# Low weight halves added from HBM one unit earlier, and input stacks moved from GpSimd's queue to SyncE's

## The chip, the cores and the metric

One core of a Trainium2 chip runs the whole kernel. The metric is device time in microseconds (us), the median of three runs. A profiled execution, taken beside them, gives the trace.

## The reference, cut to what matters

A trunk of two layers works on 272 tokens (16 learned meta tokens and 256 of the input) of width 1024, in float32:

```
for l in range(2):
    h = h + 0.5 * swiglu(rmsnorm(h, g_ffn1[l]), w1_gate[l], w1_up[l], w1_down[l])   # width 2816
    z = rmsnorm(h, g_mix[l]) @ w_in[l]            # u, q, k, v, forget logits, gates
    y_a = s5_mixer(u, ...)                        # 32 groups of 16 channels, 64 complex states each
    y_b = forgetting_attention(q, k, v, f_logit)  # 8 heads of 64
    merged = gates_a * (y_a @ w_br_a[l]) + gates_b * (y_b @ w_br_b[l])
    h = h + merged @ w_o[l]
    h = h + 0.5 * swiglu(rmsnorm(h, g_ffn2[l]), w2_gate[l], w2_up[l], w2_down[l])
return rmsnorm(h[:, 16:], g_final)
```

In s5_mixer each group of 16 channels of u is multiplied by the complex matrices B, runs through a diagonal recurrence over the 272 tokens, and is multiplied by C; then come a gelu and a gated projection.

## The kernel before

Tokens lie along the free dimension, 272 columns; the width lies in blocks of 128 partitions. Every product with a weight is made of three passes of float32r matmuls: a weight tile w is split into hi = round(w) and lo = w - hi, activations likewise, and `unit` issues hi\*hi (L309), hi\*lo (L310) and lo\*hi (L311) for each of 8 blocks of the contraction. Weights are read once, as a stream of 378 units, 189 a layer, most of 128 x 1024 numbers. A unit is thus 24 matmuls.

The class `Weights` feeds the stream. `load` issues a transfer of one unit into a `raw` tile (four of them) from SyncE's queue (SP). `high` has ScalarE copy raw into a rounded `wh` tile (five). `low` makes the `wl` tile (four): VectorE subtracts (L182), or, for every second unit from 70 to 110 of a layer save the small unit 72, 20 a layer (`by_dma`), ScalarE writes -hi (L177) and GpSimd's queue (POOL) issues a transfer that adds raw to it from SBUF (L178).

The order of the work is written out: every engine and queue takes its instructions in the order of the program. After each unit `tick` runs: `W.high()` for the unit four ahead, then whatever was put off to this tick with `later`, then `W.low()` for the unit three ahead, then a piece of a background generator, measured out by a credit per tick (`budget`). Closures in `mids` are run inside the next unit, before its seventh block.

A layer is FFN, mixer, FFN. In the mixer, units 68 to 71 make u, 72 the forget logits, 73 to 76 v, 77 to 84 k and q, 85 to 100 the gates (with the attention between them), 101 and 102 two of branch b, 103 to 106 the gated projection, 107 to 112 the rest of both branches, 113 to 120 the output projection.

`have_u` scales a block m of u (four of them), splits it into uh and ul, and `done` builds an input stack x: for each quarter q (32 rows) three transfers of 32 x 272 numbers from SBUF to SBUF, uh, ul and uh below each other (L776), twelve a block and 48 a layer, all on POOL. Stack m is ready for use (`us[m]`) two ticks later for m = 0. The background generator `ssm_branch` asks for the product of step j (16 of them; j = 4m + q) with the state weights: `bu(j)`, two matmuls (L656) with 96 rows. Bs holds B rounded in its first 64 rows and B - round(B) in its last 32. VectorE then turns, scans and turns back (L678, L731, L733, L743), and `out_m` (L668) multiplies four steps with C.

`ssm_tables`, the background work of the FFN before, fills Bs in four parts of 1024 columns: a load of B from SP, copies of the first 64 rows and the rounded last 32 on ScalarE, and a subtraction on VectorE (L563), which takes 1200 of the credit. `halves` is a pool of 19 SBUF slots of 128 x 4 x 272 numbers, which activations, stacks and intermediate results take and give back in the order of the program.

Of the kernel before, what the change touches and what calls it, by code (L numbers as in the profile page):

```python
# [15 lines left out]
P = 128  # L16
# [23 lines left out]
WARM = 10  # L40
START = 8
BLOCK = 1024
DMA_LOW = (2 * NF + 3 * KD + 1, 2 * NF + 3 * KD + 43)
BROWS = 96
DELAY = 2
MASKED = -float(2.0 ** 100)
O_U, O_Q, O_K, O_V, O_F, O_G = 0, 512, 1024, 1536, 2048, 2056
MAGIC = 12582912.0
# [82 lines left out]
class Weights:  # L131
# [17 lines left out]
    def high(self, parts=1):  # L149
        i, nc = self.nh, self.nc  # L150
        if i >= len(WHERE):
            return
        b, c, w = WHERE[i]
        while self.nb <= min(b + RAW - 1, len(BLOCKS) - 1):
            self.load()
        r = self.raw[b][:, c : c + w]
        hi = self.pool.tile([P, D], F32R, tag="wh", name=f"wh{i}", bufs=LEAD + 1)
        for c in range(0, w, w // parts):
            nc.scalar.copy(hi[:, c : c + w // parts], r[:, c : c + w // parts])  # L159
        self.part[i] = (hi, r)  # L160
        self.nh += 1

    @staticmethod
    def by_dma(i):
# [4 lines left out]
    def low(self, parts=1):  # L169
        i, nc = self.nl, self.nc  # L170
        if i >= len(WHERE):
            return
        w = WHERE[i][2]
        hi, r = self.part[i]
        lo = self.pool.tile([P, D], F32R, tag="wl", name=f"wl{i}", bufs=LEAD)
        if self.by_dma(i):
            nc.scalar.activation(lo[:, :w], hi[:, :w].bitcast(F32), AF.Copy, scale=-1.0)  # L177
            nc.gpsimd.dma_start(lo[:, :w], r, accum_op=ALU.add)  # L178
            parts = 0
        for c in range(0, w, w // parts) if parts else ():  # L180
            k = slice(c, c + w // parts)
            nc.vector.tensor_sub(lo[:, k], r[:, k], hi[:, k].bitcast(F32))  # L182
        self.part[i] = (hi, lo)
        self.nl += 1
# [7 lines left out]
def body(tc, nc, ins, out):  # L192
    v, s, pe = nc.vector, nc.scalar, nc.tensor

    with (
# [7 lines left out]
    ):  # L203
        names = iter(range(10**6))

        halves = Slots(mp, "m", 19, [P, 4, T])
        banks = Slots(pp, "ps", 6, [P, 512])
        temps = Slots(tp, "t", 6, [P, T])
        bank, tmp = banks.take, temps.take
# [1 line left out]
        def big(n, dt=F32):  # L211
            return Tiles(halves, n, dt)
# [30 lines left out]
            return par[:, c : c + n]  # L243


        state = {"tick": 0, "bg": None, "credit": 0.0, "budget": FFN_BUDGET}
        queue, tails, mids = [], [], []
        tail = tails.append

# [299 lines left out]
        def ssm_tables(l):  # L549
# [2 lines left out]
            top = BROWS - 32  # L552
            for j in range(0, NJ, 4):
                x = Bs[:, j : j + 4].rearrange("p j c -> p (j c)")
                slots = halves.take(), halves.take(F32R)
                raw, hi = (y.rearrange("p a t -> p (a t)")[:BROWS, : 8 * P] for y in slots)
                nc.sync.dma_start(raw, ins["B"][l][:, j * 2 * P : (j + 4) * 2 * P])
                yield -1
                yield -1
                s.copy(x[:top], raw[:top])  # L560
                s.copy(hi[top:], raw[top:])
                yield -1
                v.tensor_sub(x[top:], raw[top:], hi[top:].bitcast(F32))  # L563
                yield 1200
                halves.give(*slots)
            cslot = halves.take()
            Cm = cslot.rearrange("p a t -> p (a t)")[:, : 2 * NJ * 32].rearrange("p (r j c) -> p r j c", r=2, j=NJ)
            nc.sync.dma_start(Cm, ins["C"][l])
# [80 lines left out]
        def ssm_branch(l, us, yr, t0):  # L649
            n = T - t0  # L650

            def bu(j):
                pb = bp.tile([P, 2, 512], F32, tag="b2", name=f"bu{next(names)}")
                m, q = divmod(j, 4)
                for r in range(2):
                    pe.matmul(pb[:, r, :T], lhsT=Bs[:, j, r * P : r * P + P], rhs=us[m](q)[:BROWS], start=True, stop=True)  # L656
                if q == 3:
                    us[m].give()
                return pb

            def out_m(m, qt):
                ps = bank()
                for x, row, a, b, start, stop in (
                    (0, 0, t0, T, True, False), (0, 3, t0, TS, False, False), (3, 2, t0, TS, False, False),
                    (1, 3, TS, T, False, False), (2, 2, TS, T, False, False), (2, 1, t0, T, False, True),
                ):
                    for q in range(4):
                        pe.matmul(  # L668
                            ps[32 * q : 32 * q + 32, a - t0 : b - t0], lhsT=Cx[:, x, 4 * m + q, :],
                            rhs=qt[q][:, row, a:b], start=start, stop=stop,  # L670
                        )
                return ps

            def turn(dst, x, j):

                d = dst.rearrange("p (k r) t -> p k r t", k=2)
                for a, tab in ((0, E[:, :, j, 1:][:, :, ::-1]), (TS, E[:, :, j, :TS])):
                    v.tensor_tensor(  # L678
                        d[:, :, :, a : a + TS], x[:, :, a : a + TS].unsqueeze(1).to_broadcast([P, 2, 2, TS]),
                        tab.unsqueeze(2).to_broadcast([P, 2, 2, TS]), ALU.mult,  # L680
                    )
                    yield 635

            pbs = {}

            def ask(j):
                mids.append(lambda: pbs.__setitem__(j, bu(j)))

            def shut(m, qt):


                def finish():
                    if not banks.free:
                        mids.append(finish)
                        return
                    ps = out_m(m, qt)
                    halves.give(*qt)

                    def store():
                        y = yr(m)[:, t0:]  # L700
                        v.scalar_tensor_tensor(y, y, pc("d", l, m), ps[:, :n], ALU.mult, ALU.add)
                        stored.append(m)
                        banks.give(ps)

                    later(1, store)

                mids.append(finish)

            while 0 not in us:
                yield -1  # L710
            ask(0)
            g, qt = None, []
            for j in range(NJ + 1):
                back = iter(())
                if j < NJ:
                    p = buf("p", 1, [P, 4, T])
                    while j not in pbs:
                        yield -1
                    yield from turn(p, pbs.pop(j)[:, :, :T], j)
                    if j + 1 < NJ:  # L720
                        assert (j + 1) // 4 in us
                        ask(j + 1)
                if j:
                    while not halves.free:
                        yield -1
                    qt.append(halves.take())
                    back = turn(qt[-1], g, j - 1)
                    yield next(back)
                if j < NJ:
                    c, d = (x.rearrange("p r (s t) -> p (r s) t", s=2) for x in (p[:, :2], p[:, 2:]))  # L730
                    v.tensor_add(c[:, 1:3], c[:, 1:3], d[:, 3::-3])  # L731
                    yield 352
                    v.tensor_sub(c[:, 0::3], c[:, 0::3], d[:, 2:0:-1])  # L733
                    yield 352
                yield from back
                if j and j % 4 == 0:
                    shut(j // 4 - 1, qt)
                    qt = []
                if j < NJ:
                    g = buf("g", 1, [P, 2, T])  # L740
                    mg = ssm["mag"][:, l * NJ + j : l * NJ + j + 1].to_broadcast([P, T])
                    for r in range(2):
                        v.tensor_tensor_scan(g[:, r], mg, p[:, r], 0.0, ALU.mult, ALU.add)  # L743
                        yield 352
# [7 lines left out]
        def mixer(l, hh, hl, t0, finish):  # L752
# [15 lines left out]
            def have_u(ps, m):  # L768

                scaled(ps, yr(m), 0)  # L770

                def done():
                    x = big(4, F32R)
                    for q in range(4):
                        for i, part in enumerate((uh, ul, uh)):
                            nc.gpsimd.dma_start(  # L776
                                x(q)[32 * i : 32 * i + 32].bitcast(F32), part(m)[32 * q : 32 * q + 32].bitcast(F32)
                            )
                    later(DELAY if m == 0 else 0, lambda: us.__setitem__(m, x))
                    if m == 3:  # L780
                        uh.give()
                        ul.give()

                split(uh(m), ul(m), yr(m), done)

# [272 lines left out]

            bias(0)
            yb = None  # L1060
            gB, gA = big(8), None
            for i in range(16):
                state["budget"] = GATE_BUDGET if i < 11 else LATE_BUDGET
# [16 lines left out]
                later(1, e)  # L1080
                if 5 <= i < 12 and i % 2 == 1:
                    yb = yb or big(8, F32R)
                    values((i - 5) // 2)
                if 3 <= i < 11:
                    flip(i - 3)
# [372 lines left out]
```

## Time and profile before

| | |
|---|---|
| median of three runs | 1267.73 us (1265.53 to 1271.29) |
| profiled execution | 1266.69 us, of which the span is 1264.9 |
| granted clock of TensorE, mean | 0.975 |
| TensorE, busy | 1202.2 us, 95% |
| VectorE, busy | 894.1 us, 71% |
| ScalarE, busy | 682.9 us, 54% |
| GpSimd, busy | 88.0 us, 7% |
| read from HBM | 198.75 MB, 158 GB/s over the span |

Shares are means over stages that differ: the three FFN stretches keep TensorE at 100%, the mixers don't. A mixer lies at about 208 to 451 us, and again at 848 to 1072.

### The profile page before, as it was taken

The page shows a single profiled execution, that of the slowest core. Times are in us where ns is not written, and L with a number is a line of the kernel's source. Part 1 is how long each engine was busy: PE and PEld are TensorE (multiplying, and loading weights), DVE is VectorE, ACT ScalarE, POOL GpSimd, SP SyncE. Part 2 cuts the span into 40 slices and gives each one's busy share as a digit, 9 for nine tenths or more (in the row PEclk, how much of TensorE's full clock was granted, in tenths as well). Part 3 has the DMA queues.
Part 4 walks back from the last instruction along what each step waited for, and adds up shares of the span by engine and source line. Part 5 has one row for each costly group of instructions (what it writes and reads, how often), then busy time and mean ns, then how long its engine had stood idle before and what let it go on. Part 6 is the DMA issues. An engine that isn't in the chain of part 4 may idle for free.

```text
span 1264.9 us, 24220 instructions
## 1 busy us (share of the span) xinstructions
PE 1202.2 (95%) x9753; PEld 1178.7 (93%) x9753; DVE 894.1 (71%) x1682; ACT 682.9 (54%) x1092; POOL 88.0 (7%) x148
## 2 busy tenths in 40 slices
PE   9999999589997999999999999996899889999997
PEld 8999999588887999999999999996888789999997
DVE  6967899379885867989665555554797867766553
ACT  7555444446766556544454444445467665544542
POOL 0000000710010000000000000008000000000000
PEclk9999999789998999999999999997899999999999
DMA  6766555677567656655556565555766675655561
GB/s 235 210 204 207 172 171 139 163 195 185 140 166 183 189 186 208 196 168 170 172 174 187 169 179 161 182 164 160 196 184 166 168 201 183 202 185 191 176 185 63
DMA packets 65921, 225.70 MB, mean 178 GB/s; under 512 B 8560, under 2 KB 8944, under 8 KB 65808
## 3 DMA queue, kind: packets, MB, share of 16 engines
q1 hardware_dynamic: 56480, 199.06, 49.9%
q0 software_dynamic: 8912, 24.47, 10.1%
q8 instruction: 76, 1.25, 0.4%
q10 hardware_dynamic: 416, 0.62, 0.1%
q14 instruction: 37, 0.30, 0.1%
HBM read 198.75 MB, written 1.05 MB: 158 GB/s over the span
## 4 chain that ended last, share of the span: by engine, by line
PE 81%; DVE 7%; DMA 5%; issue 3%; POOL 2%; ACT 1%; SPq 0%; DVEq 0%; POOLq 0%; ACTq 0%
PE ps L311 26%; PE ps L309 26%; PE ps L310 25%; DMA wl<-raw 3%; POOL m L776 2%; DMA raw<-wts 1%; DVE wl L182 1%; DVE g L743 1%; DMA m<-m 1%; DVE m L678 1%; DVE p L678 1%; PE ps L668 1%; PE ps L976 1%; PE bu L656 0%; DVE p L731 0%
## 5 line engine op out<-in xcount | busy, mean ns | idle before, releaser
L311 PE MATMUL ps<-m,wl 128*128 128x272 f32 (+2 forms) x2960 | 858.0, 290 | 47.2 <-DMA wl<-raw 45.8
L309 PE MATMUL ps<-m,wh 128*128 128x272 f32 (+2 forms) x2960 | 860.0, 291 | 0.4 <-ACT wh L159 0.4
L310 PE MATMUL ps<-m,wh 128*128 128x272 f32 (+2 forms) x2960 | 853.3, 288 | 0.3
L159 ACT CAST wh<-raw 128x1024 fp32r<-128x1024 f32 (+2 forms) x380 | 388.9, 1024 | 446.7 <-issue 211.5
L311 PEld LDWEIGHTS ps<-m,wl 128*128 128x128 f32 (+1 forms) x2960 | 563.4, 190 | 50.8 <-DMA wl<-raw 48.3
L309 PEld LDWEIGHTS ps<-m,wh 128*128 128x128 f32 (+1 forms) x2960 | 563.5, 190 | 5.4 <-issue 3.3
L310 PEld LDWEIGHTS ps<-m,wh 128*128 128x128 f32 (+1 forms) x2960 | 563.2, 190 | 1.2 <-DVE m L345 0.7
L182 DVE TENSOR_TENSOR wl<-raw,wh 128x1024 fp32r<-128x1024 f32 (+2 forms) x340 | 401.8, 1182 | 60.0 <-PE ps L311 41.3
L178 POOL DMA_DIRECT2D wl<-raw x40 | 34.9, 882 | 912.5 <-ACT wl L177 781.5
L402 DVE TENSOR_TENSOR t<-t,ps 128x272 f32<-128x272 f32 (+1 forms) x88 | 38.1, 433 | 76.3 <-PE ps L311 73.6
L678 DVE TENSOR_TENSOR p<-bu,E 128x544 f32<-128x544 f32 x64 | 44.3, 721 | 46.1 <-PE bu L656 43.6
L396 DVE TENSOR_TENSOR t<-ps,rstd 128x272 f32<-128x272 f32 (+1 forms) x88 | 38.3, 435 | 41.3 <-PE ps L311 40.7
L776 POOL DMA_DIRECT2D m<-m x96 | 47.8, 548 | 26.5 <-ACT m L325 18.5
L678 DVE TENSOR_TENSOR m<-g,E 128x544 f32<-128x544 f32 x64 | 45.9, 718 | 0.1
L743 DVE TENSOR_TENSOR_SCAN g<-ssm_mag,p 128x272 f32<-128x272 f32 x64 | 43.3, 712 | 0.9
L404 ACT CAST m<-t 128x272 fp32r<-128x272 f32 (+1 forms) x88 | 36.2, 411 | 13.6 <-DVE t L402 13.4
L397 ACT ACTIVATE t<-t 128x272 f32<-128x272 f32 (+1 forms) x88 | 37.2, 423 | 9.2 <-DVE t L396 8.7
L177 ACT ACTIVATE wl<-wh 128x1024 fp32r<-128x1024 f32 x40 | 42.1, 1052 | 0.0
L407 DVE TENSOR_TENSOR m<-t,m 128x272 fp32r<-128x272 f32 (+1 forms) x88 | 38.0, 432 | 3.8 <-ACT m L404 3.7
L430 DVE TENSOR_TENSOR t<-ps,rstd 128x272 f32<-128x272 f32 (+1 forms) x32 | 14.0, 437 | 37.7 <-PE ps L311 37.7
L342 ACT ACTIVATE m<-h,par 128x272 fp32r<-128x272 f32 (+1 forms) x48 | 24.5, 518 | 10.8 <-DVE h L432 5.3
L345 DVE SCALAR_TENSOR_TENSOR m<-h,par,m 128x272 fp32r<-128x272 f32 (+1 forms) x48 | 23.4, 494 | 8.3 <-ACT m L342 8.2
(220 smaller groups left out, 695.2 us busy)
## 6 DMA issues: line engine op xcount, KB each, us to landing
raw<-wts SPq DMA_DIRECT2D x344, 512.0 KB, 3.9
wl<-raw POOLq DMA_DIRECT2D x40, 512.0 KB, 5.3
raw<-wts SPq DMA_DIRECT2D x32, 384.0 KB, 3.1
m<-m POOLq DMA_DIRECT2D x96, 34.0 KB, 2.8
m<-B SPq DMA_DIRECT2D x8, 384.0 KB, 5.2
h<-hT SPq DMA_DIRECT2D x4, 272.0 KB, 5.4
m<-C SPq DMA_DIRECT2D x2, 512.0 KB, 4.5
out<-m SPq DMA_DIRECT2D x2, 256.0 KB, 2.1
```

The lines of the kernel that those rows point to most:

```text
L159: nc.scalar.copy(hi[:, c : c + w // parts], r[:, c : c + w // parts])
L177: nc.scalar.activation(lo[:, :w], hi[:, :w].bitcast(F32), AF.Copy, scale=-1.0)
L182: nc.vector.tensor_sub(lo[:, k], r[:, k], hi[:, k].bitcast(F32))
L309: pe.matmul(ps[:width, :n], lhsT=a, rhs=mh, start=first and i == ks[0], stop=False)
L310: pe.matmul(ps[:width, :n], lhsT=a, rhs=ml, start=False, stop=False)
L311: pe.matmul(ps[:width, :n], lhsT=b, rhs=mh, start=False, stop=last and i == ks[-1])
L396: v.tensor_mul(x[:, :n], pg[:, :n], rstd[:, t0:])
L402: v.tensor_mul(y[:, :n], y[:, :n], pu[:, :n])
L407: v.tensor_sub(al(f)[:, t0:], y[:, :n], ah(f)[:, t0:].bitcast(F32))
L678: v.tensor_tensor(d[:, :, :, a : a + TS], x[:, :, a : a + TS].unsqueeze(1).to_broadcast([P, 2, 2, TS]), tab.unsqueeze(2).to_broadcast([P, ...
L743: v.tensor_tensor_scan(g[:, r], mg, p[:, r], 0.0, ALU.mult, ALU.add)
L776: nc.gpsimd.dma_start(x(q)[32 * i : 32 * i + 32].bitcast(F32), part(m)[32 * q : 32 * q + 32].bitcast(F32))
```

## The change

- `high` makes the low half of the 40 units of `by_dma` at once, one tick earlier than `low` did; the added operand comes from the weights in HBM and no longer from raw. `low` passes over such a unit. There are five wl tiles in place of four.
- The stack transfers go out on SP. `put` issues three for one quarter, and the quarters of a block are spread over ticks by `STACKS`; uh and ul are given back with the last quarter. A quarter is ready for use one tick after its issue, and `us` goes by step j.
- The last 32 rows of Bs are -round(B), written by ScalarE, with B added from HBM by a transfer on POOL; the subtraction, its credit and one slot go.
- `halves` has 18 slots; from the gates' start until yb is taken, the generator leaves two free.

```diff
+LOWS = LEAD + 1
-DELAY = 2
+DELAY = 1
+STACKS = (0, 1, 4, 7)
@@ Weights.high
         self.nh += 1
+        if self.by_dma(i):
+            lo = self.pool.tile([P, D], F32R, tag="wl", name=f"wl{i}", bufs=LOWS)
+            nc.scalar.activation(lo[:, :w], hi[:, :w].bitcast(F32), AF.Copy, scale=-1.0)
+            off, n = BLOCKS[b]
+            src = self.dram[off * P : (off + n) * P].rearrange("(p n) -> p n", p=P)
+            c = WHERE[i][1]
+            nc.gpsimd.dma_start(lo[:, :w], src[:, c : c + w], accum_op=ALU.add)
+            self.part[i] = (hi, lo)
@@ Weights.low
+        if self.by_dma(i):
+            self.nl += 1
+            return
-        lo = self.pool.tile([P, D], F32R, tag="wl", name=f"wl{i}", bufs=LEAD)
-        if self.by_dma(i):
-            nc.scalar.activation(lo[:, :w], hi[:, :w].bitcast(F32), AF.Copy, scale=-1.0)
-            nc.gpsimd.dma_start(lo[:, :w], r, accum_op=ALU.add)
-            parts = 0
+        lo = self.pool.tile([P, D], F32R, tag="wl", name=f"wl{i}", bufs=LOWS)
@@ body
-        halves = Slots(mp, "m", 19, [P, 4, T])
+        halves = Slots(mp, "m", 18, [P, 4, T])
@@ ssm_tables
-                slots = halves.take(), halves.take(F32R)
+                slot = halves.take()
                 s.copy(x[:top], raw[:top])
-                s.copy(hi[top:], raw[top:])
+                s.activation(x[top:], raw[top:], AF.Copy, scale=-1.0)
+                nc.gpsimd.dma_start(x[top:], src[top:], accum_op=ALU.add)
+                halves.give(slot)
                 yield -1
-                v.tensor_sub(x[top:], raw[top:], hi[top:].bitcast(F32))
-                yield 1200
-                halves.give(*slots)
@@ ssm_branch
-                        assert (j + 1) // 4 in us
+                        while j + 1 not in us:
+                            yield -1
-                    while not halves.free:
+                    while len(halves.free) <= state["keep"]:
@@ mixer
+                def put(q, x):
+                    for i, part in enumerate((uh, ul, uh)):
+                        nc.sync.dma_start(
+                            x(q)[32 * i : 32 * i + 32].bitcast(F32), part(m)[32 * q : 32 * q + 32].bitcast(F32)
+                        )
+                    later(DELAY, lambda: us.__setitem__(4 * m + q, x))
+                    if q == 3 and m == 3:
+                        uh.give()
+                        ul.give()
                 def done():
                     x = big(4, F32R)
+                    first = state["tick"]
                     for q in range(4):
-                        for i, part in enumerate((uh, ul, uh)):
-                            nc.gpsimd.dma_start(
-                                x(q)[32 * i : 32 * i + 32].bitcast(F32), part(m)[32 * q : 32 * q + 32].bitcast(F32)
-                            )
-                    later(DELAY if m == 0 else 0, lambda: us.__setitem__(m, x))
-                    if m == 3:
-                        uh.give()
-                        ul.give()
+                        at = first + (q // 2 if m == 0 else q) + STACKS[m]
+                        queue.append((at, lambda q=q: put(q, x)))
             bias(0)
+            state["keep"] = 2
                     yb = yb or big(8, F32R)
+                    state["keep"] = 0
```

## Rows read from the trace of the kernel before

**Rows 1.** The page: busy time of each engine, share, instructions.

```profile
PE 1202.2 (95%) x9753; PEld 1178.7 (93%) x9753; DVE 894.1 (71%) x1682; ACT 682.9 (54%) x1092; POOL 88.0 (7%) x148
```

**Rows 2.** Waits of TensorE, whole span: waiter <- releaser, us in total, times, longest.

```profile
PE ps L311 <- DMA wl<-raw: 45.8, 11, 14.0
...
PE bu L656 <- DVE p L678: 1.5, 2, 0.8
```

**Rows 3.** The first of these waits at 200:300, 300:420, 840:900 and 900:1050 us.

```profile
PE ps L311 <- DMA wl<-raw: 18.6, 2, 14.0
...
PE ps L311 <- DMA wl<-raw: 6.8, 2, 3.4
...
PE ps L311 <- DMA wl<-raw: 13.6, 2, 9.8
...
PE ps L311 <- DMA wl<-raw: 6.7, 5, 2.1
```

**Rows 4.** Windows of 8 us after a stall, first and last of seven (PEclk before DMA share).

```profile
243.20:251.20 8.00, 7.98 (x44) 7.98 (x45) 3.43 (x6) 2.29 (x3) 7.03 (x15) 0.65 0.48 130
...
1026.70:1034.70 8.00, 7.44 (x48) 7.24 (x48) 4.82 (x11) 3.69 (x6) 0.86 (x1) 0.79 0.78 199
```

**Rows 5.** Timeline of POOL, 200 to 256 us: adding transfers of units 74 and 76.

```profile
238.04 0.91 POOL L178 DMA_DIRECT2D wl<-raw  x1 [0.25 <-issue]
...
252.75 1.83 POOL L178 DMA_DIRECT2D wl<-raw  x2 [0.21 <-issue]
```

**Rows 6.** Timeline of ScalarE: copy and negation of units 74 and 108; three sigmoids.

```profile
217.62 1.05 ACT L159 CAST wh<-raw 128x1024 fp32r<-128x1024 f32 x1 [1.02 <-DMA raw<-wts]
...
224.75 1.05 ACT L177 ACTIVATE wl<-wh 128x1024 fp32r<-128x1024 f32 x1
...
389.46 1.05 ACT L159 CAST wh<-raw 128x1024 fp32r<-128x1024 f32 x1 [3.04 <-PE ps L310]
...
391.25 1.35 ACT L1101 ACTIVATE m<-m,par 128x272 f32<-128x272 f32 x3 [0.45 <-DVE m L1100]
...
394.06 1.04 ACT L177 ACTIVATE wl<-wh 128x1024 fp32r<-128x1024 f32 x1
```

**Rows 7.** Timeline of POOL: the adding transfer of unit 108.

```profile
395.50 0.86 POOL L178 DMA_DIRECT2D wl<-raw  x1 [10.47 <-ACT m L1101]
```

**Rows 8.** Transfers: count, KB, median us to landing; below, the range for wl.

```profile
raw<-wts SPq DMA_DIRECT2D x344, 512.0 KB, 3.9
wl<-raw POOLq DMA_DIRECT2D x40, 512.0 KB, 5.3
...
m<-m POOLq DMA_DIRECT2D x96, 34.0 KB, 2.8
...
DMA to landing us min/median/max: 4.5/5.3/8.8
```

**Rows 9.** Timeline of SP at the start: two issues back to back.

```profile
1.65 0.90 SPq L224 DMA_DIRECT2D h<-hT  x2
```

**Rows 10.** Windows: length, busy us of PE, PEld, DVE, ACT, POOL, then PEclk.

```profile
210.90:218.30 7.40, 7.40 (x58) 7.21 (x57) 7.06 (x21) 3.27 (x4) 0.60 (x1) 1.00 0.48 116
262.65:283.00 20.35, 20.35 (x165) 20.29 (x164) 16.97 (x30) 12.77 (x22) 2.58 (x3) 1.00 0.70 183
229.00:378.80 149.80, 128.84 (x1119) 119.50 (x1117) 111.30 (x207) 89.88 (x183) 32.77 (x55) 0.92 0.65 167
660.00:680.00 20.00, 20.00 (x160) 20.00 (x160) 12.47 (x19) 10.28 (x16) 0.00 (x0) 1.00 0.69 215
```

**Rows 11.** VectorE: its wait for the stack products; the state weights' subtraction (xcount | busy, mean).

```profile
DVE p L678 <- PE bu L656: 43.6, 8, 16.5
...
L563 DVE TENSOR_TENSOR Bs<-m,m 32x1024 fp32r<-32x1024 f32 x8 | 9.7, 1218 | 11.1 <-ACT m L561 11.0
```

**Rows 12.** Timeline: VectorE makes ul of blocks 0 and 1; TensorE starts unit 73.

```profile
223.26 0.79 DVE L328 TENSOR_TENSOR m<-m,m 128x272 fp32r<-128x272 f32 x2
...
225.65 0.37 PE L309 MATMUL ps<-m,wh 128*128 128x272 f32 x1
```

More of the change, by code (lines that the diff above doesn't have):

```diff
@@ L172, in low @@
             return
+        if self.by_dma(i):
+            self.nl += 1
+            return
         w = WHERE[i][2]
         hi, r = self.part[i]
-        lo = self.pool.tile([P, D], F32R, tag="wl", name=f"wl{i}", bufs=LEAD)
-        if self.by_dma(i):
-            nc.scalar.activation(lo[:, :w], hi[:, :w].bitcast(F32), AF.Copy, scale=-1.0)
-            nc.gpsimd.dma_start(lo[:, :w], r, accum_op=ALU.add)
-            parts = 0
-        for c in range(0, w, w // parts) if parts else ():
+        lo = self.pool.tile([P, D], F32R, tag="wl", name=f"wl{i}", bufs=LOWS)
+        for c in range(0, w, w // parts):
             k = slice(c, c + w // parts)
@@ L243, in pc @@
             return par[:, c : c + n]
-        state = {"tick": 0, "bg": None, "credit": 0.0, "budget": FFN_BUDGET}
+        state = {"tick": 0, "bg": None, "credit": 0.0, "budget": FFN_BUDGET, "keep": 0}
         queue, tails, mids = [], [], []
@@ L554, in ssm_tables @@
                 x = Bs[:, j : j + 4].rearrange("p j c -> p (j c)")
-                slots = halves.take(), halves.take(F32R)
-                raw, hi = (y.rearrange("p a t -> p (a t)")[:BROWS, : 8 * P] for y in slots)
-                nc.sync.dma_start(raw, ins["B"][l][:, j * 2 * P : (j + 4) * 2 * P])
+                slot = halves.take()
+                raw = slot.rearrange("p a t -> p (a t)")[:BROWS, : 8 * P]
+                src = ins["B"][l][:, j * 2 * P : (j + 4) * 2 * P]
+                nc.sync.dma_start(raw, src)
                 yield -1
@@ L655, in bu @@
                 for r in range(2):
-                    pe.matmul(pb[:, r, :T], lhsT=Bs[:, j, r * P : r * P + P], rhs=us[m](q)[:BROWS], start=True, stop=True)
+                    pe.matmul(pb[:, r, :T], lhsT=Bs[:, j, r * P : r * P + P], rhs=us[j](q)[:BROWS], start=True, stop=True)
                 if q == 3:
-                    us[m].give()
+                    us[j].give()
                 return pb
```

## The prediction

> **What bounds the kernel now.** I read the page first: TensorE is busy 95% of the span [rows 1], so what can be won lies in the 5% and in the clock. Next came what TensorE waits for. Nearly all of it is one thing, the low half of a weight that an adding transfer makes: 45.8 us in 11 waits; the next in question, the state product waiting for VectorE, has 1.5 [rows 2]. Split by stretch, the waits lie in the mixers only: 18.6 us where the first begins, 6.8 where it ends, 13.6 and 6.7 in the second [rows 3]. Then the clock behind these waits. Behind seven of the eleven waits TensorE resumes at a granted clock of 0.50, its 1.2 GHz level, and is back at 2.4 GHz some us later: over the 8 us behind each the mean is 0.61 to 0.79 [rows 4]. One minus it, summed over the seven, is 2.20, so work at half speed cost 2.20 x 8 = 17.6 us. Elsewhere it is 1.00 [rows 10]. Waits and clock together are 63.4 us, the most that this cause can give back.
>
> Why is the transfer late? At the start, unit 74's ScalarE part ends at 225.8 (224.75 + 1.05) [rows 6], but POOL issues the addition at 238.04, and unit 76's at 252.75 [rows 5]: between stand stack transfers in the order of the program, 24 of them in these 14.7 us, 0.6 us each. POOL is busy 7% over the span, and yet its order is the bound there. At the mixer's end POOL is free. Unit 108's copy ends at 390.5, its negation waits in ScalarE's order until 394.06 [rows 6], POOL issues at 395.50 [rows 7], and a landing takes 4.5 to 8.8 us [rows 8]; TensorE got there 3.4 us too early.
>
> **The additions one unit ahead.** No instruction is added on ScalarE: a negation (1.05 us) follows its copy instead of standing a tick later. For unit 108 that is 394.06 - 390.5 = 3.6 us earlier, as long as its stall; for unit 74 it is 224.75 - 218.67 = 6.1 us. What it costs when the cover is gone: a unit lasts 24 x 20/160 = 3.0 us at full clock [rows 10], and the copy four units ahead starts when its wh tile is free, so landing is due 4 x 3.0 = 12 us on. Copy, negation and 0.4 us to the issue take 2.5, leaving 9.5 us for a landing, above the 8.8 that was the longest. Reading HBM instead of SBUF has no row. A plain load of the same size lands in 3.9, an addition from SBUF in 5.3 [rows 8]; I take 5.3, between 3.9 and 8.8. raw is released by the copy and not by the landing, so weights come earlier. That is worth nothing by itself, since copies are ahead already: unit 74's ended at 218.67, and TensorE, in unit 73 from 225.65 [rows 12], reached it 3.0 us later, 10 us behind the copy. The fifth wl tile keeps the negation from waiting for the unit in work.
>
> At the mixer's end two things can still be late. ScalarE there does gate sigmoids between the copies: in a tick a copy (1.05), half a negation (0.5) and three sigmoids (1.35) [rows 6] are 2.9 us of TensorE's 3.0, before the activations of the projection itself. Once TensorE no longer stalls, ScalarE falls behind there, and the slack is 9.5 less a landing: 4.2 at the median, 0.7 at the slowest. Bounds: 0, and the 6.8 us of that stage's stall coming back. I take 2 us a layer, nearer to the median's side, 4 in all.
>
> **The stacks on SP.** POOL loses 96 issues and keeps 40, plus eight for the state weights, each beside an idle queue, so the stalls at the starts (18.6 + 13.6) go altogether. SP gains 48 issues a layer. An issue there takes 0.45 us (two in 0.90 [rows 9]), so 21.6 us, spread over 13 ticks of 3.0 = 39 us: three a tick beside one weight load, 1.8 us of 3.0; nine in one tick, where it falls 1.5 us behind. Behind a stack in SP's order stand the weight loads, and behind them the copies, with their 10 us. A stack's data are ready by then (uh and ul of block 0 at 224.05 [rows 12]), except in the first tick. The wait that is added is the first product's, in unit 73 in place of 74. It stands before the seventh block, 225.65 + 0.75 x 3.0 = 227.9 [rows 12]; three issues from 224.05 and a landing of 2.8 [rows 8] make 228.2. So 0.3 us, or 6 if it lands like the slowest addition (8.8); below nothing it can't go, since nothing waited there. I take 1 a layer, 2 in all. Behind that product stand all later matmuls.
>
> At this place a rule of the Trainium skill speaks against the change: in DMA: Bandwidth & Descriptors, section Queues, rings and completion order, transfers of one issuer's queue are taken in ring order by each DMA engine, while different queues are served in turn. By it a stack on SP lands behind the 512 KB load ahead of it, not beside it as POOL's did: 3.9 + 2.8 = 6.7 us instead of 2.8, 3.9 us lost a layer and 1221 in all. No row of before shows a small transfer behind a load on SP.
>
> **VectorE without the stall.** The stall gave VectorE time. Its wait for the products is 43.6 us, 16.5 of it in one piece at the stall [rows 11]. From 229.0 to 378.8 it is busy 111.3 of 149.8 us [rows 10]; without the stall and its clock (18.6 + (0.35 + 0.31) x 8 = 23.9) the stretch is 125.9 us and VectorE 88% full. It worked at 16.97/20.35 = 83% in the part just behind the stall [rows 10]. If it can't be packed tighter, the stretch is 111.3/0.834 = 133.5, 7.6 us lost; if it can, 0. I take 3 a layer, 6 in all, since the pace there was TensorE's.
>
> **State weights and slots.** Eight subtractions of 1.22 us [rows 11] leave VectorE in FFN stretches in which TensorE is full; worth 0 there. But 4 x 1200 credits at 1000 a tick bring the tables almost five ticks forward. In the first layer their rest runs after the FFN, 7.06 of 7.4 us [rows 10], and delays the subtraction of unit 71 and the first splits: about 4 us less VectorE work, some 1 us of TensorE's time. Counted tick by tick, 18 slots suffice: uh and ul are held ten ticks longer, at least one slot stays free, and the generator finds one each time. It is one tick ahead of before, so its last step falls under the gates. Value 0; a step pushed out behind the gates would cost its turns and scans, unhidden.
>
> **The sum.** Profiled execution 1266.69 (span 1264.9 and 1.8 around it) - 63.4 + 4 + 2 + 6 - 1 = 1214.3; the median shown is 1.0 above that execution, so 1215.
>
> **Rivals.**
> 1. VectorE becomes the mixers' bound. For it: 83% behind the stall. Against: only 1.5 us of TensorE's waits were for it. Price 7.6 a layer in place of 3, and ScalarE's end at its bound, (6.8 + 6.7) in place of 4: 1215 + 9 + 9.5 = 1234. Chance 0.16.
> 2. Additions from HBM land late, at 12 us instead of 5.3. Then each four units at full pace lose 12 - 9.5 = 2.5; some 22 of a layer's units run at 3.0 us, so 5.5 x 2.5 = 14 a layer, and about as much again in half clock: 1215 + 55 = 1270 at worst, about 1243 with the clock kept. For it: the landings stretch to 8.8 already. Against: a plain load from HBM is the quickest of the large transfers [rows 8]. Chance 0.06.
> 3. Slower: SP as the new bound. If each stack holds SP until something lands, h us instead of 0.45, its tick of three is longer than a unit from h = (3.0 - 0.4)/3 = 0.87, and 96 x (h - 0.87) is added; the gain of 52 is eaten from h = 1.41. With h = 2.8, a whole landing [rows 8], it adds 185: 1400. Against: SP's transfers were issued 0.45 apart with no landing between [rows 9]. Chance 0.04.
> 4. It doesn't do what it says: the negations move, but ScalarE's own order, not POOL's, holds the additions. Then the starts' waits alone go, 32.2 + 11 of clock, and VectorE takes its 6 and gives its 1: 1230. Against: 12 us between negation and issue at unit 74. Chance 0.06.
>
> **How the numbers follow.** The forecast has 0.68: 1203 (all 63.4 won) to 1230. For 8 in 10 the range takes in rivals 4 and 1 and goes up to 1241; down it ends at 1201, a little under all 63.4, for small waits that go too (the 1.5 us of [rows 2]). A measurement of this kernel can't tell less than 0.5%, 6.3 us, from no change; only rival 3 and the far end of 2 get there: faster 0.94, no change 0.02, slower 0.04.
>
> **What would show it.** In the changed profile: POOL's adding transfers within 1 us of their negations; the wait of L311 for wl below 6 us; PEclk 1.00 through the mixers; SP's stack issues about 0.45 us apart; a wait of the first state product (L656) for a stack, 0 to 6 us. I am wrong if copies (L159) wait for raw longer than before, if TensorE waits for VectorE's L678 by tens of us, or if landings of wl pass 9.5 us.

## The result, and the profile after

The changed kernel takes 1208.99 us (median of four runs, 1208.77 to 1212.64), the kernel before beside it 1269.51; the ratio is 0.953, with an interval of 0.950 to 0.957. Forecast were 1215, in a range of 1201 to 1241. The profiled execution took 1209.21 us, with a span of 1207.4 and a mean granted clock of 0.995, so 57.5 us less than that of before.

Lines have moved: L309, L310 and L311 are now L318, L319 and L320, the negation is L166, the adding transfer L170, the stacks' transfer L784, the state product L665. First the page's busy times, which answer to [rows 1]:

```profile
PE 1186.9 (98%) x9753; PEld 1165.2 (97%) x9753; DVE 879.7 (73%) x1674; ACT 686.0 (57%) x1092; POOL 47.2 (4%) x60
```

TensorE's idle time fell from 62.7 us (1264.9 - 1202.2) to 20.5 (1207.4 - 1186.9), by 42.2, and its busy time by 15.3 at the same count of instructions; 14.2 of that is the half clock (17.6 before, 3.4 now, below). What it waits for now, against [rows 2]:

```profile
PE bu L665 <- DMA m<-m: 4.6, 2, 2.3
PE ps L318 <- DVE t L1166: 3.8, 4, 1.4
...
PE ps L320 <- DVE wl L191: 0.4, 2, 0.2
```

The 45.8 us for the low halves that the adding transfers make are gone, all of them. Two waits are new: the first state product of each layer for its stack, and the start of products with the gated branch's output (L1166, behind a sigmoid), two a layer at the mixer's end. Next, units 74 and 76 on ScalarE (copy L161, negation L166), and then their adding transfers on POOL, against [rows 5, 6]:

```profile
217.26 1.06 ACT L166 ACTIVATE wl<-wh 128x1024 fp32r<-128x1024 f32 x1
...
222.15 1.06 ACT L166 ACTIVATE wl<-wh 128x1024 fp32r<-128x1024 f32 x1
```

```profile
218.68 0.88 POOL L170 DMA_DIRECT2D wl<-wts  x1 [9.89 <-ACT m L334]
223.61 0.86 POOL L170 DMA_DIRECT2D wl<-wts  x1 [4.05 <-ACT m L334]
```

The first stands 0.4 us behind the end of its negation (218.32), the second as well (223.21); before, unit 74's stood 12 us behind. SP's stack issues in the same stretch, and what one of them waits for between 218 and 240:

```profile
219.78 4.02 SPq L784 DMA_DIRECT2D m<-m  x6
...
228.09 7.31 SPq L784 DMA_DIRECT2D m<-m  x9
...
236.08 1.78 SPq L784 DMA_DIRECT2D m<-m  x3
```

```profile
SPq L784 <- DMA raw<-wts: 3.6, 1, 3.6
```

Three issues take 1.78 us, 0.59 each. Ahead of the nine SP stands still: for 3.6 us, up to 228.09, a stack issue waits until a weight load has landed, though the data of its block had been there since the first issue at 219.78. The transfers and their landings, against [rows 8]; the range below is that of wl:

```profile
raw<-wts SPq DMA_DIRECT2D x344, 512.0 KB, 3.7
wl<-wts POOLq DMA_DIRECT2D x40, 512.0 KB, 7.2
...
m<-m SPq DMA_DIRECT2D x96, 34.0 KB, 5.0
```

```profile
DMA to landing us min/median/max: 5.2/7.2/9.1
```

An addition from HBM lands in 7.2 us, not in the 5.3 of one from SBUF. The longest here, 9.1, is below the 9.5 that the prediction left for it; in a second profile of the same kernel ("the changed kernel again" below) the longest is 9.7, and TensorE has no wait for these low halves there either. Last, windows, as in [rows 4, 10] (length, busy us of PE, PEld, DVE, ACT, POOL, PEclk, DMA share, GB/s): the 8 us behind each of the two stack waits, a stretch from 229 up to where the scan's last block is stored (356.0 now, 380.0 before), and 20 us out of it.

```profile
228.80:236.80 8.00, 8.00 (x52) 8.00 (x53) 7.23 (x13) 4.59 (x10) 0.87 (x1) 0.79 0.74 141
833.40:841.40 8.00, 8.00 (x52) 8.00 (x53) 7.26 (x13) 4.59 (x10) 0.87 (x1) 0.79 0.67 129
...
229.00:356.00 127.00, 126.63 (x1135) 118.12 (x1135) 112.32 (x210) 86.48 (x177) 12.18 (x14) 0.99 0.77 194
...
245.00:265.00 20.00, 20.00 (x184) 19.44 (x187) 19.08 (x33) 12.06 (x20) 2.62 (x3) 1.00 0.96 264
```

In the mixers half clock is left only behind the new stack waits: 2 x 0.21 x 8 = 3.4 us. VectorE does the same work up to there, 112.3 us, in 127.0; before it was 112.5 in 151.0 (229 to 380; the prediction's 111.3 of 149.8 end at 378.8).

### The profile page after: what moved, and what is told of

It reads as the page before. It is cut to its first block, busy times and chain, and to the rows that moved or that the text cites. A ratio compares the mean times of both kernels' runs of the same rounds, so it can differ in the third digit from the quotient of the medians.

```text
span 1207.4 us, 24185 instructions
## 1 busy us (share of the span) xinstructions
PE 1186.9 (98%) x9753; PEld 1165.2 (97%) x9753; DVE 879.7 (73%) x1674; ACT 686.0 (57%) x1092; POOL 47.2 (4%) x60
## 4 chain that ended last, share of the span: by engine, by line
PE 89%; ACT 5%; DVE 3%; DMA 2%; issue 1%; SPq 0%; DVEq 0%; ACTq 0%
PE ps L318 28%; PE ps L320 28%; PE ps L319 28%; DMA m<-m 1%; ACT m L1118 1%; PE ps L677 1%; ACT wh L161 1%; PE ps L991 1%; DVE wl L191 1%; PE bu L665 1%; DMA raw<-wts 1%; DVE g L753 0%; ACT wl L166 0%; ACT L1070 0%; DVE m L687 0%
## 5 line engine op out<-in xcount | busy, mean ns | idle before, releaser
L318 PE MATMUL ps<-m,wh 128*128 128x272 f32 (+2 forms) x2960 | 855.0, 289 | 4.8 <-DVE t L1166 3.8
L320 PE MATMUL ps<-m,wl 128*128 128x272 f32 (+2 forms) x2960 | 850.9, 287 | 0.4 <-DVE wl L191 0.4
L319 PE MATMUL ps<-m,wh 128*128 128x272 f32 (+2 forms) x2960 | 848.5, 287 | 0.6
L161 ACT CAST wh<-raw 128x1024 fp32r<-128x1024 f32 (+2 forms) x380 | 388.3, 1024 | 397.6 <-issue 210.9
L318 PEld LDWEIGHTS ps<-m,wh 128*128 128x128 f32 (+1 forms) x2960 | 557.8, 188 | 11.0 <-DVE t L1166 4.6
L319 PEld LDWEIGHTS ps<-m,wh 128*128 128x128 f32 (+1 forms) x2960 | 557.6, 188 | 2.3 <-DVE m L337 1.1
L320 PEld LDWEIGHTS ps<-m,wl 128*128 128x128 f32 (+1 forms) x2960 | 557.7, 188 | 1.5 <-DVE wl L191 0.8
L170 POOL DMA_DIRECT2D wl<-wts x40 | 34.8, 871 | 737.5 <-ACT wl L166 558.6
L687 DVE TENSOR_TENSOR p<-bu,E 128x544 f32<-128x544 f32 x64 | 43.7, 720 | 16.0 <-PE bu L665 14.2
L413 ACT CAST m<-t 128x272 fp32r<-128x272 f32 (+1 forms) x88 | 36.2, 411 | 14.4 <-DVE t L411 14.2
L166 ACT ACTIVATE wl<-wh 128x1024 fp32r<-128x1024 f32 x40 | 42.4, 1061 | 1.3
L376 DVE RECIPROCAL rstd<-t 128x272 f32<-128x272 f32 (+1 forms) x6 | 11.0, 1836 | 19.8 <-ACT t L375 19.8
```

What stands on the lines that cost most here:

```text
L318: pe.matmul(ps[:width, :n], lhsT=a, rhs=mh, start=first and i == ks[0], stop=False)
L319: pe.matmul(ps[:width, :n], lhsT=a, rhs=ml, start=False, stop=False)
L320: pe.matmul(ps[:width, :n], lhsT=b, rhs=mh, start=False, stop=last and i == ks[-1])
L687: v.tensor_tensor(d[:, :, :, a : a + TS], x[:, :, a : a + TS].unsqueeze(1).to_broadcast([P, 2, 2, TS]), tab.unsqueeze(2).to_broadcast([P, ...
```

## The experiments

All are the changed kernel with one edit, unless said otherwise; the rows with a late first product and a credit have two. The ratio is to the kernel before on the same chip.

| kernel | median us | ratio, interval |
|---|---|---|
| stacks on POOL, spread | 1210.15 | 0.952 [0.950, 0.954] |
| stacks on POOL, twelve at once | 1264.70 | 0.995 [0.994, 0.997] |
| stacks on SP, twelve at once | 1265.18 | 0.996 [0.994, 0.997] |
| additions in the later tick | 1235.54 | 0.972 [0.970, 0.974] |
| additions read raw in SBUF | 1220.60 | 0.960 [0.959, 0.962] |
| state weights by VectorE | 1211.55 | 0.954 [0.952, 0.956] |
| first product a tick later | 1228.46 | 0.967 [0.965, 0.970] |
| the same, stacks on POOL | 1228.47 | 0.967 [0.965, 0.969] |
| a tick later, credit 2800 under the gates | 1213.50 | 0.957 [0.955, 0.959] |
| a tick later, credit 2000 before the gates | 1210.03 | 0.954 [0.953, 0.955] |
| that, at most six stack issues a tick | 1209.93 | 0.952 [0.950, 0.954] |
| the changed kernel again | 1209.05 | 0.953 [0.952, 0.954] |

### Which queue, or how many at once

```diff
-                        nc.sync.dma_start(
+                        nc.gpsimd.dma_start(
```

> The changed kernel, but the stack transfers go out on POOL again, spread over the ticks as in the change. Theory A (what stalled TensorE was the order: a block's twelve transfers at once ahead of an addition): with three a tick POOL has 3 x 0.5 + 0.9/2 = 2 us of work in a tick of 3.0, additions leave within 1.5 us of their negation, the wait of the low matmuls for wl stays under 2 us, and the time is 1204 to 1212. Theory B (the queue: POOL's issues are too slow, SP was needed): additions leave 3 us or more late, wl waits of 10 us or more return, 1220 or more. Beside it, for the first state product: if a stack landed 8.5 us after its issue because it stood behind weight loads in SP's ring, on POOL it lands in about 3 and the product's 2.3 us a layer go; if the transfer engines were just full, it still waits.

Measured 1210.15 us: to the time, the queue is of no account once the stacks are spread. Not all additions left within 1.5 us of their negation: unit 78's stood behind stacks for 3.4 us in the first layer and 4.5 in the second, which cost TensorE one wait of 0.8. In TensorE's waits the one for the stack stays, on POOL's queue as on SP's:

```profile
PE bu L665 <- DMA m<-m: 4.3, 2, 2.2
...
PE ps L320 <- DMA wl<-wts: 0.8, 1, 0.8
```

The two bursts (the one on POOL has the edit above as well):

```diff
-                    later(DELAY, lambda: us.__setitem__(4 * m + q, x))
+                    later(2 if m == 0 else 0, lambda: us.__setitem__(4 * m + q, x))
...
-                        at = first + (q // 2 if m == 0 else q) + STACKS[m]
-                        queue.append((at, lambda q=q: put(q, x)))
+                        put(q, x)
```

On POOL:

> The changed kernel, but the stacks go out on POOL, a block's twelve at once, as before the change; the additions stay one unit ahead and read HBM. Theory A: unit 74's addition now leaves before the stacks, unit 76's behind two or three blocks of them (12 to 18 us), so one stall of 4 to 8 us at each mixer's start with 2.5 us of half clock behind it: 1220 to 1230, wl waits 8 to 16 us. Theory C (the additions' lead alone did it): no wl wait, 1205 to 1212.

On SP:

> The other corner beside the burst on POOL (0.995 of before): all twelve transfers of a block at once, on SP. Theory A (what harmed was POOL's order, in which the additions stood behind the stacks): on SP the weight loads are delayed by 12 x 0.6 = 7.1 us a block, less than the 10 us by which copies are ahead, so the stalls for wl stay under 10 us and the time is 1210 to 1230 (with the L677 waits of 12.6 us that the burst on POOL showed, since use begins a tick later too). Theory B (a burst is bad on either queue): loads behind it are late, copies (L159 of before, L161) wait for raw, TensorE waits for wh or wl by over 20 us, and the time is 1245 to 1270.

Both came out far slower than the first theory's figure, and both within 0.5% of the kernel before; SP's 1265.18 lies where its second theory had it, though what waits there are ScalarE's copies and not the low halves. TensorE's waits on POOL, then on SP (there L884 is the transposes of v and L878 ScalarE's copy ahead of them):

```profile
PE ps L320 <- DMA wl<-wts: 36.6, 6, 11.7
PE ps L677 <- DVE m L687: 12.6, 4, 4.7
```

```profile
PE ps L884 <- ACT P L878: 31.9, 6, 7.4
PE ps L677 <- DVE m L687: 12.7, 4, 4.7
...
PE ps L320 <- DMA wl<-wts: 0.7, 1, 0.7
```

On POOL the additions stand behind the stacks, as before the change, only a unit later, since unit 74's is now issued ahead of them. On SP, the low halves are in time, but the weight loads are not. SP's own timeline and ScalarE's, in that kernel:

```profile
217.29 2.43 SPq L147 DMA_DIRECT2D raw<-wts  x3
219.81 19.80 SPq L784 DMA_DIRECT2D m<-m  x24
239.71 0.54 SPq L147 DMA_DIRECT2D raw<-wts  x1
```

```profile
244.20 1.04 ACT L161 CAST wh<-raw 128x1024 fp32r<-128x1024 f32 x1 [12.16 <-DMA raw<-wts]
245.15 0.38 ACT L878 COPY P<-ps 128x272 f32<-128x272 f32 x1
```

The 24 issues take 19.8 us, but not all of it is issuing. What SP's stack issues wait for, over the whole span:

```profile
SPq L784 <- DMA raw<-wts: 7.6, 2, 4.1
```

After eight issues SP stands still for 4.1 us, until 228.43, for a weight load to land; the rest is 15.7 us, 0.65 each. What makes an issue wait for that load was not tested. The next load stands behind all 24, the weight's copy waits 12.2 us for raw, and behind it in ScalarE's order stands the copy that TensorE needs. So a burst holds up whatever shares the queue with it. My expectation for SP reckoned with one block of twelve issues and 0.6 us each; two blocks came together, and the wait for a landing came on top.

### The additions: a tick earlier, and from HBM

The negation and its addition put back into `low`'s tick, the source still in HBM:

```diff
@@ Weights.high
-        if self.by_dma(i):
-            lo = self.pool.tile([P, D], F32R, tag="wl", name=f"wl{i}", bufs=LOWS)
...
@@ Weights.low
+            nc.gpsimd.dma_start(lo[:, :w], src[:, c : c + w], accum_op=ALU.add)
+            self.part[i] = (hi, lo)
             self.nl += 1
             return
```

> The changed kernel, but negation and addition are made in the tick of the low half again, not one unit ahead; HBM source and stacks on SP stay. Theory A: the lead shrinks from 12 to about 9 us where units run at 3.0 us, less 2.5 before the issue leaves 6.5 for landings of 5.2 to 9.1: waits for wl of 5 to 15 us in all, at the mixers' ends above all (6.8 and 6.7 before), 1220 to 1235. Theory D (moving the stacks alone did it): wl waits under 3 us, 1207 to 1213.

Measured 1235.54, just above what was expected: some 26 us hang on the earlier tick. The wait is twice the 5 to 15 us that I gave it, with 18.4 us at the mixers' ends and 10.0 at their starts. TensorE waits for the low halves in 14 places:

```profile
PE ps L318 <- DMA wl<-wts: 28.4, 14, 5.8
```

With the source in SBUF, still a tick early:

```diff
-            off, n = BLOCKS[b]
-            src = self.dram[off * P : (off + n) * P].rearrange("(p n) -> p n", p=P)
-            c = WHERE[i][1]
-            nc.gpsimd.dma_start(lo[:, :w], src[:, c : c + w], accum_op=ALU.add)
+            nc.gpsimd.dma_start(lo[:, :w], r, accum_op=ALU.add)
```

> The changed kernel, but the addition reads raw in SBUF again, one unit ahead. If the HBM source is what made an addition land in 7.2 us in place of 5.3, it lands in about 5.3 here; if the crowded transfer engines (busy 0.9 to 1.0 in the starts) did, it stays at 6.5 or more. Theory A: the time hangs on order and lead, not on the source: 1205 to 1213. Theory E (raw given back early is what won the time): copies wait for raw up to 8 us longer, TensorE's waits pass 15 us, 1225 or more.

Measured 1220.60, between the two. What SP's weight loads wait for between 212 and 230, and TensorE's longest wait:

```profile
SPq L147 <- DMA wl<-raw: 12.4, 2, 6.4
```

```profile
PE bu L662 <- DMA m<-m: 10.1, 2, 5.1
```

A raw tile is free only when its addition has landed; the load into it waits on SP, and the first stack, issued at 219.8 in the changed kernel, waits behind that load until 226.7. That wait is 5.5 us longer than in the changed kernel, and TensorE's busy time 4.2 us longer at the same count of matmuls (the clock is 0.62 and 0.75 over the 8 us behind the two waits): together 9.7 of the 12.8 us between the two profiled executions. The other 3 us, small waits for ScalarE, were not traced further. Reading HBM makes each landing longer (7.2 against 5.7 here) and is yet worth 11 us, most of it because raw comes free with the copy.

### The state weights

```diff
...
-                s.activation(x[top:], raw[top:], AF.Copy, scale=-1.0)
-                nc.gpsimd.dma_start(x[top:], src[top:], accum_op=ALU.add)
-                halves.give(slot)
+                s.copy(hi[top:], raw[top:])
                 yield -1
+                v.tensor_sub(x[top:], raw[top:], hi[top:].bitcast(F32))
+                yield 1200
+                halves.give(*slots)
```

> Only the state weights are undone: their last 32 rows are made by VectorE as before, with the 1200 of the credit four times a layer. The prediction's value is 1 us: time 1209 to 1211, with a wait for the low half of unit 71 or later first splits. The rival: the four ticks that the tables come later push the generator behind the FFN, and the mixer's first products and the scan's end with it: 1214 or more, with waits of TensorE for VectorE in the mixers.

Measured 1211.55, just above what was expected, so about 2 us for this part, and its interval (0.952 to 0.956) holds the changed kernel's 0.953: it can't be told from nothing.

### The first product's wait

What are the 4.6 us and the 3.4 of half clock behind them worth? The first product a tick later, with the stacks on SP, and on POOL:

```diff
-                    later(DELAY, lambda: us.__setitem__(4 * m + q, x))
+                    later(DELAY + (m == 0 and q < 2), lambda: us.__setitem__(4 * m + q, x))
```

> Question: what the wait of the first state product costs. In the changed kernel it is 4.6 us in two pieces of 2.3, and the granted clock is 0.80 in the 8 us behind the first. Here the first two quarters of block 0 are ready a tick later, so the first product is asked in unit 74, 3.0 us on. Theory A (the wait and its half clock are a plain loss, and the chain of the scan has a tick to spare): both go, 4.6 + about 3.5 us, and the time is 1201 to 1204. Theory B (the generator has no tick to spare, as in the burst kernel, where it slipped past the gates): TensorE waits for the last turns of the scan (L677) at the mixers' ends, 4 us or more a layer, and the time is 1212 to 1222.

> The same delay with the stacks on POOL's queue, spread as in the change. If the queue is of no account once the stacks are spread, this is within 3 us of the kernel with the same delay on SP: 1201 to 1207 (or 1212 to 1222 if the scan slips past the gates). If POOL's second job, the additions, still suffers from the stacks (in the spread kernel on POOL units 76 and its like left POOL 3.4 and 4.5 us late), TensorE waits for wl by 0.8 us or more, and the time is 3 to 8 us above that kernel.

Neither waits for the stack, and both take 19 us more, beyond the ranges given; by mechanism it is the second theory. On POOL the low halves are waited for 4.2 us, on SP 4.9, so the queue makes no difference here either. In the kernel on SP the wait for the last turns of the scan appears:

```profile
PE ps L677 <- DVE m L687: 12.6, 4, 4.7
PE ps L320 <- DMA wl<-wts: 4.9, 5, 1.4
```

```profile
352.00:360.00 8.00, 3.31 (x23) 2.14 (x21) 7.93 (x18) 4.87 (x8) 0.00 (x0) 0.91 0.22 76
360.00:368.00 8.00, 6.67 (x64) 5.15 (x65) 3.82 (x9) 4.92 (x7) 0.88 (x1) 0.66 0.79 190
```

In the first window (columns as above) TensorE has 3.3 us of work and VectorE 7.9: the scan's last step no longer falls under the gates, and half clock follows. That is also in the two bursts, which begin a tick later too. Against the kernels with the same late first product a burst costs 36.2 us on POOL (1264.7 - 1228.5) and 36.7 on SP; the rest of its loss is the tick.

The tick's credit given back under the gates (2800, the last five 2700), or before them (2000 for 1800), both with the later first product on SP:

```diff
-GATE_BUDGET = 2700.0
-LATE_BUDGET = 2600.0
+GATE_BUDGET = 2800.0
+LATE_BUDGET = 2700.0
```

> The kernel with the first product a tick later took 1228.5 us, 19 above the changed kernel; its trace has 12.6 us of waits for the last turns of the scan. Counted by credits, a tick later costs 1800, and the scan's last step is pushed out behind the gates. Here that delay stays, and the credit of a tick under the gates is 2800 (last five 2700) in place of 2700 (2600): counted, the last step then falls under the gates again. Theory A (the credits are the cause of the 19 us): L677's waits go, the wait for the stack (4.6 us) and the half clock behind it stay gone, and the time is 1201 to 1206, below the changed kernel. Theory B (VectorE has no room for 100 ns more a tick, or the later start itself is what costs): TensorE waits for VectorE's turns or for the low halves it makes, and the time is 1212 or more.

```diff
-QKV_BUDGET = 1800.0
+QKV_BUDGET = 2000.0
```

> The same with the credit added where VectorE is fullest: 2000 in place of 1800 in a tick of the units before the gates (73 to 84), where it is busy 92 to 96% in the changed kernel. If VectorE's load is a bound there (the first rival of the prediction), its subtractions come late and TensorE waits for wl or for the score products: 3 us or more above the kernel with more credit under the gates. If not, both are alike within 2 us.

> The changed kernel again, on the same chip as the two others: 1207 to 1212 us, so that differences of 3 us to it can be told.

1213.50, 1210.03 and 1209.05. L677's waits are gone in both, so the credits were the cause of most of the 19 us; but neither beats the changed kernel, and the expected 1201 to 1206 was wrong, as was the guess that more credit before the gates costs over 3 us against the other. In the second, what TensorE waits for, and ScalarE's order around it:

```profile
PE ps L885 <- ACT P L879: 4.3, 2, 2.3
```

```profile
239.99 1.05 ACT L161 CAST wh<-raw 128x1024 fp32r<-128x1024 f32 x1 [6.53 <-DMA raw<-wts]
...
242.78 0.36 ACT L879 COPY P<-ps 128x272 f32<-128x272 f32 x1
```

The stack's wait is gone, and 14 us later another of the same size stands there. Its cause seemed to be SP: nine stack issues in one tick ahead of the load (5.81 us in that kernel, behind a wait of 3.6 for a landing). So they were spread to six at most; the edit is shown against the kernel with 2000:

```diff
-STACKS = (0, 1, 4, 7)
+STACKS = (0, 2, 5, 7)
...
-                    later(DELAY + (m == 0 and q < 2), lambda: us.__setitem__(4 * m + q, x))
+                    later(DELAY + (m == 0 and q < 1), lambda: us.__setitem__(4 * m + q, x))
...
-                        at = first + (q // 2 if m == 0 else q) + STACKS[m]
+                        at = first + ((q + 1) // 2 if m == 0 else q) + STACKS[m]
```

> The kernel with 2000 of credit won the 5 us of the stack's wait and lost them to a new one: transposes waiting for ScalarE's copy of v (4.3 us, and half clock behind). In ScalarE's order that copy stands behind the copy of a weight, which waited 6.5 us for raw, whose load stood on SP behind 15 stack issues in 9.7 us, nine of them in one tick. Here the issues are spread to at most six a tick (three, six, three, three for block 0, block 1 a tick later, block 2 as well); delay and credit stay. Theory A (SP's issues hold the load): the load goes out 1.9 us or more earlier, L885's wait falls under 1 us, the half clock goes, and the time is 1201 to 1206, below the changed kernel's 1209.05 (ratio to before 0.947 to 0.951, from 0.953). Theory B (the transfer engines are full there, 0.94 to 1.05 over 248 to 280, and loads are late in whatever order they are issued): the wait for raw stays, and the time is 1207 to 1212.

L885's wait went to nothing, as the first theory had it, and the time came out as the second had it: 1209.93, a ratio of 0.952 [0.950, 0.954], no different from the changed kernel. The wait has moved once more, to the state product (first line, the whole span). The profile names no releaser for it, but the two other lines do: VectorE's turn of the product before, out of the one buffer that the kernel has for these products, ends at 260.31 (258.96 + 1.35), and the next product starts 0.1 us later; at 251.77 it is the same.

```profile
PE bu L665 <- issue: 3.9, 4, 1.6
...
258.96 1.35 DVE L687 TENSOR_TENSOR p<-bu,E 128x544 f32<-128x544 f32 x2
...
260.41 0.49 PE L665 MATMUL bu<-m,Bs 96*128 96x272 f32 x2 [1.64 <-issue]
```

The 20 us around these places, and the sum of the five windows from 205 to 305:

```profile
245.00:265.00 20.00, 17.57 (x158) 16.61 (x160) 19.53 (x34) 12.07 (x18) 2.62 (x3) 1.00 0.99 248
...
sum 100.00, PE 96.78 PEld 91.94 DVE 86.16 ACT 66.85 POOL 12.65; mean PE 19.36 PEld 18.39 DVE 17.23 ACT 13.37 POOL 2.53
```

VectorE is busy 19.5 of 20 us, and the transfer engines' share is 0.99. The same sum for the changed kernel run again, and for the one with 2000 of credit:

```profile
sum 100.00, PE 96.81 PEld 92.27 DVE 84.70 ACT 66.64 POOL 12.62; mean PE 19.36 PEld 18.45 DVE 16.94 ACT 13.33 POOL 2.52
```

```profile
sum 100.00, PE 96.75 PEld 92.03 DVE 84.75 ACT 65.78 POOL 12.63; mean PE 19.35 PEld 18.41 DVE 16.95 ACT 13.16 POOL 2.53
```

TensorE is idle 3.2 us of these hundred in all three kernels: from 226.5 on in the changed one, from 241 with the credit, at 251 and 259 with the spreading. Two causes have been taken away in turn and a third of the same size appeared: right behind the stack stand VectorE and the transfers, both nearly full from 245 on. The spreading did keep the clock at 1.00 in this stretch, where the two others fall to 0.91 and 0.93 over 20 us; by the clock that is 1.6 to 1.8 us, which the time doesn't show: over the whole span TensorE is idle 22.0 us with the spreading (1208.2 - 1186.2) and 20.8 in the changed kernel (1207.9 - 1187.1). Whether VectorE or the transfers would hold alone was not separated. No version beat the changed kernel.

## Why the prediction was right

The cause and its size were right: of the 63.4 us that wl's waits and their half clock were put at, 57.5 came out as net gain. What was given back was put at 11 us and measured 5.9 (63.4 - 57.5). By its steps:

- **The additions one unit ahead.** All 45.8 us went, and their half clock. POOL issues 0.4 us behind the negation, as the step had it, and the earlier tick alone is worth 26 us. The landing was mis-sized (7.2 instead of 5.3). The 9.5 of slack is no sharp bound: 9.7 in the second profile cost nothing, and with the stacks spread on POOL the longest landing was 10.9 and the waits 0.8 in all. "That is worth nothing by itself", said of raw's earlier release, failed: it is worth 11 us, most of it by way of SP's order, in which a load that waits for raw holds up the stack behind it.
- **The stacks.** The stalls at the starts went altogether, as put. But "each beside an idle queue" names the wrong half of the edit: moved to SP in a burst they cost as much as on POOL, and spread on POOL they cost 1 us more than on SP, less than the intervals tell apart. The spreading is what the gain hangs on.
- **SP's price** of 0.45 us an issue was too low: the median is 0.59 in the changed kernel. The nine in one tick took 7.31 us there, 6.30 in its second profile and 5.81 with 2000 of credit, so 0.65 to 0.81 each, below the 0.87 from which rival 3 counts. What the argument against rival 3 had wrong is "with no landing between": once in each mixer's start a stack issue does wait for a landing, 3.6 and 3.9 us in the changed kernel. In the burst that wait and 24 issues together made SP the bound of its stretch.
- **The first product's wait** was put at 2 us in all and measured 4.6 with 3.4 of half clock behind it, 8.0. It is one of the two terms that failed by 6 us: the landing taken was the median of a quiet row, 2.8, and the first three took 7.6 to 8.5. By the rule cited of the Trainium skill (DMA: Bandwidth & Descriptors, section Queues, rings and completion order) it would have been 3.9 more a layer; the trace has 2.3 and 1.7 of clock. That isn't proof of ring order: on POOL's queue the first stacks landed in 8.0 to 8.3, but an addition stood ahead of them there too, and the transfer engines' share, as the view gives it, was 1.02 on SP's queue and 1.03 on POOL's between 220 and 228. The runs leave open which it is.
- **The mixers' ends**, put at 4 us, cost 3.8, but not as a late low half: TensorE waits there for VectorE's product (L1166) behind a sigmoid, one step on in the same crowd on ScalarE.
- **VectorE**, put at 6 us, cost nothing: its 112.3 us fit into 127.0, 88%, close to the packed case of 125.9. Small waits of before for the scan and its turns went too: the rest of TensorE's idle time fell by 4.8 us (42.2 - 45.8 + 4.6 + 3.8).
- **State weights**, put at a gain of 1 us, lie within what can be measured.

So the give-back is 8.0 + 3.8 - 4.8 - 1.1 = 5.9; the last is what the busy time fell beyond 17.6 - 3.4. Two terms missed by 6 us each, the first product's wait upwards and VectorE downwards; that they cancelled is luck. The 6 us between the forecast of 1215 and the 1209 measured are the small gains that it left out.

Of the rivals, the bound on VectorE did not show in the changed kernel, but it may be next: once the stack is in time, TensorE is held for as long where VectorE and the transfers are nearly full. The late additions did not come: the longest landing of the changed kernel was 9.7, against rival 2's 12. Rival 4, ScalarE's order, is answered by the 0.4 us between negation and issue.

## What to carry to other kernels

Ask of every queue what stands behind a burst in it, not only which queue is idle: moving a block's twelve transfers to the other queue gained nothing, spreading them over ticks gained 36 us. A merged row of issues can hide a wait: look at what the queue waits for before taking its length as a price. A buffer that is released by a fast reader rather than by a slow transfer is worth something at the far end of the queue that refills it. And a wait of a few us that sits in front of two nearly full resources is not a gain in waiting; look at their busy share in that stretch before taking it away.

## What the runs showed of the hardware

An adding transfer of 512 KB landed in 7.2 us from HBM and 5.7 from SBUF, where a plain load took 3.7. Issues of 34 KB transfers on SP took 0.59 us at the median (0.51 to 1.71) in the changed kernel, and 0.52 on POOL (0.50 to 0.87) with the same spreading. In a row of them SP stood still for 3.6 us (changed kernel) and 4.1 us (burst) until a weight load had landed, with the data of the transfer long ready. Over 20 us in the first mixer's start the transfer engines' share was 0.96 at 264 GB/s (changed kernel) and 0.99 at 248 (six issues a tick); every second unit there is read from HBM twice.
